# Second mixer of a two-layer step: order of the projections, and its two attentions in one alternating pipeline

## The chip, the core and the metric

The kernel runs on one core of a Trainium2 chip. The core has a matrix engine (TensorE, PE, with its weight loads PEld), a vector engine (VectorE, DVE), a scalar engine with lookup functions (ScalarE, ACT), a general engine (GpSimd, POOL) and an engine that mostly issues transfers (SyncE, SP). Each runs its own instructions in a fixed order and waits for the others through semaphores. The metric is the device time of one execution in microseconds, taken as the median of repeated runs.

## What is computed

One step of a hybrid backbone with two layers, in float32, on 384 tokens of width 1024: 128 prompt tokens, which see only each other, and 256 sample tokens, which see a cached context of 128 keys and themselves. Layer 0 mixes with windowed attention (A) and a gated scan (B); layer 1, which the change touches, mixes with latent attention (C) and with attention over normalised queries and keys (D). Behind each mixer stand an output projection with a residual layer norm and a SwiGLU feed-forward. The second mixer, cut from the reference:

```python
def mixer_cd(h, ...):
    cq, ckv, kpe, qd, kd, vd = jnp.split(h @ w_in, ODD_SPLIT, axis=-1)   # 384, 256, 32, 512, 256, 256
    qc = (rms_norm(cq, g_cq) @ w_q_up).reshape(bsz, l, 8, 64 + 32)
    ckv = rms_norm(ckv, g_ckv)
    qd = rms_norm(qd.reshape(bsz, l, 8, 64), g_dq)
    kd = rms_norm(kd.reshape(bsz, l, 4, 64), g_dk)
    # sample tokens: rotary on qc's last 32, kpe, qd, kd; context of 128 cached tokens appended to latents, keys, values
    # C: keys and values of 8 heads from (ckv @ w_kv_up), kpe shared by the heads; scores over 96 dimensions
    # D: 8 query heads of 64 on 4 key/value heads
    oc, od = dense_gqa(qc, kc, vc), dense_gqa(qd, kd, vd)    # softmax(q k^T * scale) v
    return jnp.concatenate([oc, od], -1) @ w_out
```

## The kernel before

**Precision.** A float32 product of a projection is made by three matmuls: each operand is split into a high and a low part (`wh`, `wl` of weights, `hH`, `hL` of activations). `mm3` (L126 to L129) issues high by high, low weight by high, high by low. `wload` (L113 to L124) loads a block of weights (`wr`, three buffers), makes `wh` on ACT (L122) and `wl` on DVE (L123; three buffers each). Scores, products with V and transposes are single float32 matmuls.

**Tiling.** The 384 tokens are three tiles of 128: tile 0 is the prompt, 1 and 2 the sample. A projection of n columns (`proj_all`) keeps one accumulator per token tile in PSUM and runs over the 1024 inputs in eight blocks: 72 matmuls of n columns each. PSUM has eight banks: four for `pst` (scores, transposed probabilities, D's query accumulators), three for `pjt` (projections, transposes of keys and latents), one for `pat` (products with V).

**The second mixer** (`mixer_cd`, from L1240). `acc0`, the projection of D's keys and values, comes in finished or nearly so from the boundary before it. Then, in program order:
- `acc1`, the projection of D's queries (512 columns).
- `evac_dkv` (L1282) of each tile: squares and their sum, 1/rms by a power on POOL (L110), the normalised key (L1287), for sample tiles the rotation (a product on POOL, L752; on DVE a product, L754, and an add that also doubles each head, L758), then four transposes `tk` (`turn_k`, L794), whose copies go to `kD`.
- `d_ctx`: the cached keys and values of D.
- `evac_dq` (L1295): copy, squares, rotation, four transposes `tq`, copy into `qD`; the query's 1/rms goes into the scale of the exponentials.
- the query latent, 384 columns (`proj_tm` with `evac_cq`: copy and squares on ACT, L1354 and L1355, three transposes, gain, split), and the kv latent, 288 columns (`c_ctx_`, `evac_ckv`, transposes `tl`).
- `kv_up` (keys and values of C from its latents), D's attention, `q_up` (queries of C, two halves of four heads, with the transposes `tqc`, L1405), C's attention, and `out_first`, the first half of the output projection on 512 columns.

**The attention** (L725) yields five units: one for the prompt, and one for each of four pairs of heads over the two sample query tiles. A sample unit has two parts. `pair_1` makes four score tiles of 128x384 in the `pst` banks (L722 for D, L1411 for C), their maxima (DVE, L640), exponentials with row sums (ACT, L643), reciprocals, and scales the probabilities by them (POOL, L650). `pair_2` transposes twelve blocks (L673), copies them out (L656), makes six products with V (L679) and splits the result into `hH` and `hL`. The second part of a unit is issued behind the first part of the next one.

**What sets the order.** The instructions of each engine are placed by a scheduler, which follows the program and a priority. `with ahead(part)` moves the priority of all that it encloses by the number of `part` in the table `AHEAD` (L30): a positive number moves it ahead. So pieces of D's attention (`attD`, 100) and of `q_up` (1000) stand among the projections around them. Work tiles come from pools (`Slots`): `qS` holds query buffers of 1536 columns, two of them before; `qD` takes one for the whole mixer, and the two halves `qT` of C's queries need one each.

Of the kernel before, what the change touches and what calls it, by code (L numbers as in the profile page):

```python
# [21 lines left out]
D = 1024  # L22
# [4 lines left out]
GRID_W = 64  # L27
NEG = -1e30

AHEAD = {"w": 1500, "w0": -700, "lv0": 1000, "lv1": 800, "attA": 1500, "attC": 400, "attD": 100, "fin": 500, "qs": -1500,  # L30
         "ada": -400, "ada_step": -500, "of0": -500, "of1": 1500, "ho0": 300, "ho1": 300, "gb": 100, "ib": -60,
         "kvup": 30, "cq": -200, "dctx": -100, "lat": -400, "chain": -700, "qup": 1000, "rope": 1000, "adav": -500,
         "of2": -200, "adav1": -100}

ADA = (([(0, 2), (0, 3), (0, 4)], [(0, 5, 0), (1, 0, 1), (1, 1, 0), (1, 2, 1), (1, 3, 0), (1, 4, 1)]), ([], [(1, 5, 0)]))
# [6 lines left out]
def tile_backbone_step(ctx, tc, I, O):  # L42
# [33 lines left out]
    @contextmanager  # L76
    def ahead(part, more=0):
        with tc.high_priority(offset=AHEAD[part] + more):
            yield
# [293 lines left out]
    def proj_all(w, c0, n, bank=None):  # L373
        acc, part, load = proj_parts(lambda ks: w[ks, c0:c0 + n], n, bank)
        for u in range(4):
            load(u)
            for t in range(3):
                part(t, u)
        return acc

    def proj_tm(w, c0, n, evac):
        acc = proj_all(w, c0, n)
        for t in range(3):
            evac(t, acc[t])
# [233 lines left out]

    def inv_sums(M, A, sm, nm, sink, n):
        if A.sink:  # L620
            es = M.sm.tile([P, n], F32, tag=f"es{n}", name="es")
            nc.vector.tensor_tensor(out=es.rearrange("p (a b) -> p a b", a=2), in0=nm, in1=sink, op=ALU.add)
# [6 lines left out]

    def pair_1(M, i, A):  # L630
        pr = [M.tile("pr", F32).rearrange("p (t k) -> p t k", t=2) for _ in range(2)]
# [90 lines left out]
            nc.tensor.matmul(outs[a], q[rows], k[rows], start=True, stop=stop)  # L722


    def attention(M, A):  # L725
        work = [(prompt_1, prompt_2, 0)] + [(pair_1, pair_2, i) for i in range(4)]
        prev = None
        for f1, f2, h in work:
            pr = f1(M, h, A)
            if prev:  # L730
                prev[0](M, prev[1], A, prev[2])
            prev = (f2, h, pr)
            yield
        prev[0](M, prev[1], A, prev[2])
        yield

    def drain(*gens):
        gens = list(gens)
        while gens:
            for g in list(gens):  # L740
                if next(g, 1):
                    gens.remove(g)
# [497 lines left out]
    def mixer_cd(ps1, acc0):  # L1240
        w = I["w_in_cd"][0]
        SC_D = 64 ** -0.5
        SC_C = 96 ** -0.5
        es = ExitStack()
        M = Slots(es, {"m4": (4, 1152), "u2": (3, 512), "t2": (5, 512), "one": (1, 0), "m8": (3, 2048), "qS": (2, 1536),
                       "pr": (4, 768), "pt": (6, 512), "sc": (1, 0)})
        vD = M.one.tile([P, 4, 4, 64], F32, name="vD")
        scl = {}
# [16 lines left out]
        def d_ctx():  # L1265
            kcx = dups(M, 4)
            for i in range(2):
                dma(out=kcx[0][0][:, :, i, :], in_=I["cache_d_k"][0, 0])
            dma(out=vD[:, 3], in_=I["cache_d_v"][0, 0])
            turn_k(kcx, kD, slice(384, 512), pjt)  # L1270
# [24 lines left out]
        def evac_dq(t, acc):  # L1295
            qn = M.tile("t2", F32).rearrange("p (h d) -> p h d", h=8)
            nc.scalar.activation(qn, acc.rearrange("p (h d) -> p h d", h=8), AF.Copy)
            ss = head_ss(acc, 8)
            if t:
                rope_apply(M, qn, 8, 64, tbq, t - 1, qn, False)  # L1300
            else:
                nc.vector.tensor_tensor(out=qn, in0=qn, in1=C["gdq"].unsqueeze(1).to_broadcast([P, 8, 64]), op=ALU.mult)
            turn_q(qn, qD, tok(t))
            with ahead("qs"):
                query_scale("D", t, ss, 1.0 / 64, SC_D)
# [115 lines left out]
        kT = [t8(F32, f"kT{i}") for i in range(2)]  # L1421
        latH, latL = [M.tile("m4", F32R)[:, 0:1024].rearrange("p (k n) -> p k n", k=2) for _ in range(2)]
        cqH, cqL = [M.tile("m4", F32R).rearrange("p (k n) -> p k n", k=3) for _ in range(2)]
        acc1 = proj_all(w, 672, 512, pst)
        for t in range(3):
            evac_dkv(t, acc0[t])
        d_ctx()
        for t in range(3):
            evac_dq(t, acc1[t])
        with ahead("cq"):  # L1430
            proj_tm(w, 0, 384, evac_cq)
        with ahead("lat"):
            c_ctx_()
            proj_tm(w, 384, 288, evac_ckv)
        with ahead("kvup"):
            vC = kv_up()
        with ahead("attD"):
            drain(attention(M, Att(sd_sample, sd_prompt, lambda tl, h: vD[:, tl, h // 2, :], 4,
                                   sc=scl["D"][0], nsc=scl["D"][1], nh=8, bank=pat)))
        qT = [M.tile("qS", F32).rearrange("p (h t) -> p h t", h=4) for _ in range(2)]  # L1440
        with ahead("qup"):
            q_up()
        with ahead("attC"):
            drain(attention(M, Att(sc_sample, sc_prompt, lambda tl, h: vC[:, tl, h * 64:(h + 1) * 64], 0,
                                   sc=scl["C"][0], nsc=scl["C"][1], bank=pat)))
        with ahead("of1"):
            first = out_first(I["w_out"][1], ORDER[1], keep)
# [4 lines left out]
    def ada_later(l):  # L1452
        todo = ADA[l][0]
        for i, a in enumerate(todo):
            with ahead("ada", AHEAD["ada_step"] * i):
                ada_chunk(*a)
# [79 lines left out]
```

## Time and profile before

| | |
|---|---|
| Median of three runs | 1082.47 us (1077.73 to 1084.74) |
| The profiled execution, its own time | 1080.16 us |
| Its span in the trace | 1078.3 us |
| Mean granted clock of PE | 0.989 |
| Busy: PE, DVE, ACT, POOL | 95%, 61%, 41%, 11% |

The profile is one execution. Its page gives, among others, the busy time of each engine, the chain of work that ended last, and groups of instructions by line. The trace behind it can be asked for timelines of an engine, for the busy time in chosen stretches, and for the clock that was granted to PE. A matmul counts as busy from its issue to its modelled end, so neighbours overlap in the timeline; the distance of starts is the pace. Times are counted from the span's start; the second mixer lies from about 608 to 773 us.

### The profile page before, as it was taken

The numbers are of one execution on the slowest core, as the hardware profiler recorded it, in microseconds if no ns is written. First come the engines' busy times: TensorE is split into PE (matmuls) and PEld (weight loads), VectorE is DVE, ScalarE is ACT, GpSimd is POOL, SyncE is SP. The second block draws the span as 40 slices with busy tenths as digits, with TensorE's granted clock in tenths as the row PEclk, the third lists the DMA queues.
The fourth block names the chain that finished last, engine by engine and source line by source line (L and its number), as shares of the span: only waits on it lengthen the run. The fifth ranks groups of instructions, "written<-read, shape, count | busy, mean of one in ns | idle before, by whom it ended". The sixth has DMA issues, their size and how long they took to land.

```text
span 1078.3 us, 15811 instructions
## 1 busy us (share of the span) xinstructions
PE 1023.6 (95%) x6105; PEld 865.2 (80%) x6105; DVE 657.7 (61%) x1110; ACT 440.5 (41%) x776; POOL 121.2 (11%) x166
## 2 busy tenths in 40 slices
PE   5999999997899999999999998979899999999995
PEld 4889877565799899897688776665689999998885
DVE  2589767455897477377247867656499464443337
ACT  2376746333443333232134457555163333332231
POOL 0021201210300000000001243122130000000004
PEclk8999999999999999999999999989999999999998
DMA  9873254457257777766663621144136464543331
GB/s 306 261 229 96 84 194 148 128 166 254 79 176 229 262 205 234 233 202 224 219 198 105 188 66 61 34 156 157 40 114 198 122 192 137 164 129 129 126 117 59
DMA packets 114353, 173.12 MB, mean 161 GB/s; under 512 B 9419, under 2 KB 82150, under 8 KB 114278
## 3 DMA queue, kind: packets, MB, share of 16 engines
q1 hardware_dynamic: 113526, 171.78, 50.7%
q8 instruction: 48, 0.79, 0.3%
q10 hardware_dynamic: 752, 0.34, 0.1%
q14 instruction: 27, 0.22, 0.1%
HBM read 167.84 MB, written 4.24 MB: 160 GB/s over the span
## 4 chain that ended last, share of the span: by engine, by line
PE 75%; DVE 9%; DMA 8%; issue 3%; ACT 2%; POOL 2%; SPq 0%; DVEq 0%; ACTq 0%; POOLq 0%
PE pf L129 10%; PE pf L128 10%; PE pf L127 10%; PE o L127 6%; PE o L128 6%; PE o L129 6%; DMA ar<-in_w_ada 4%; PE pj L129 3%; PE pj L127 3%; PE pj L128 3%; PE ada_acc L203 3%; DVE wl L123 2%; PE hs L883 2%; PE s L722 2%; PE ov L679 1%
## 5 line engine op out<-in xcount | busy, mean ns | idle before, releaser
L123 DVE TENSOR_TENSOR wl<-wr,wh 128x1024 fp32r<-128x1024 f32 (+4 forms) x200 | 235.9, 1182 | 239.9 <-ACT wh L122 237.1
L122 ACT ACTIVATE wh<-wr 128x1024 fp32r<-128x1024 f32 (+4 forms) x200 | 202.4, 1015 | 345.0 <-PE pf L128 123.5
L129 PE MATMUL pf<-hH,wl 128*128 128x384 f32 x688 | 232.7, 338 | 0.0
L127 PE MATMUL pf<-hH,wh 128*128 128x384 f32 x688 | 232.4, 338 | 0.0
L128 PE MATMUL pf<-hL,wh 128*128 128x384 f32 x688 | 232.4, 338 | 0.0
L129 PEld LDWEIGHTS pf<-hH,wl 128*128 128x128 f32 x688 | 129.4, 188 | 3.1 <-issue 3.1
L128 PEld LDWEIGHTS pf<-hL,wh 128*128 128x128 f32 x688 | 129.4, 188 | 2.5 <-issue 2.5
L127 PEld LDWEIGHTS pf<-hH,wh 128*128 128x128 f32 x688 | 129.4, 188 | 2.3 <-issue 2.2
L127 PE MATMUL o<-wh,aH 128*128 128x512 f32 (+1 forms) x280 | 101.3, 362 | 0.4 <-DVE a L1182 0.4
L128 PE MATMUL o<-wl,aH 128*128 128x512 f32 (+1 forms) x280 | 101.2, 361 | 0.4 <-DVE wl L123 0.4
L129 PE MATMUL o<-wh,aL 128*128 128x512 f32 (+1 forms) x280 | 101.0, 361 | 0.0
L129 PE MATMUL pj<-wh,hL 128*128 128x512 f32 (+3 forms) x240 | 88.9, 372 | 1.9 <-POOL hL L344 1.7
L127 PE MATMUL pj<-wh,hH 128*128 128x512 f32 (+3 forms) x240 | 89.2, 376 | 0.4 <-DVE vT L174 0.2
L261 DVE SCALAR_TENSOR_TENSOR part<-ar,cT,part 128x512 f32<-128x512 f32 x112 | 80.4, 747 | 13.7 <-DMA ar<-in_w_ada 13.6
L128 PE MATMUL pj<-wl,hH 128*128 128x512 f32 (+3 forms) x240 | 88.7, 370 | 0.0
L110 POOL TENSOR_TENSOR ve<-ve,nhalf 128x1 f32<-128x1 f32 x12 | 7.0, 585 | 631.7 <-DVE ve L530 370.2
L127 PEld LDWEIGHTS o<-wh,aH 128*128 128x128 f32 x280 | 52.9, 189 | 10.1 <-issue 1.4
L129 PEld LDWEIGHTS o<-wh,aL 128*128 128x128 f32 x280 | 52.8, 188 | 9.2 <-issue 1.2
L128 PEld LDWEIGHTS o<-wl,aH 128*128 128x128 f32 x280 | 52.9, 189 | 8.8 <-DVE wl L123 0.7
L129 PEld LDWEIGHTS pj<-wh,hL 128*128 128x128 f32 x240 | 45.1, 188 | 12.0 <-POOL hL L344 2.6
L127 PEld LDWEIGHTS pj<-wh,hH 128*128 128x128 f32 x240 | 44.8, 188 | 9.7 <-issue 1.9
L128 PEld LDWEIGHTS pj<-wl,hH 128*128 128x128 f32 x240 | 45.2, 188 | 7.8 <-issue 1.0
(325 smaller groups left out, 1511.5 us busy)
## 6 DMA issues: line engine op xcount, KB each, us to landing
ar<-in_w_ada SPq DMA_DIRECT2D x80, 512.0 KB
wr<-in_w_ffn_down SPq DMA_DIRECT2D x44, 512.0 KB
wr<-in_w_ffn_gate SPq DMA_DIRECT2D x40, 512.0 KB
wr<-in_w_ffn_up SPq DMA_DIRECT2D x40, 512.0 KB
wr<-in_w_in_ab SPq DMA_DIRECT2D x18, 512.0 KB
ar<-in_w_ada SPq DMA_DIRECT2D x32, 256.0 KB
wr<-in_w_out SPq DMA_DIRECT2D x16, 512.0 KB
wr<-in_w_in_ab SPq DMA_DIRECT2D x16, 256.0 KB
```

The lines of the kernel that those rows point to most:

```text
L110: nc.gpsimd.tensor_tensor(out=out, in0=v, in1=nhalf[:, :n], op=ALU.pow)
L122: nc.scalar.activation(hi, raw, AF.Copy)
L123: nc.vector.tensor_tensor(out=lo, in0=raw, in1=hi.bitcast(F32), op=ALU.subtract)
L127: nc.tensor.matmul(out, lh, rh, start=start, stop=False)
L128: nc.tensor.matmul(out, lh, rl, start=False, stop=False)
L129: nc.tensor.matmul(out, ll, rh, start=False, stop=stop)
L203: nc.tensor.matmul(acc[32 * g:32 * g + 32], st, src[:, :, g * P:(g + 1) * P], start=start, stop=stop, tile_position=(0, 32 * g))
L261: nc.vector.scalar_tensor_tensor(out=dst, in0=raw[:, j], scalar=sc, in1=dst, op0=ALU.mult, op1=ALU.add)
L679: nc.tensor.matmul(ov[64 * a:64 * a + 64], A.v(kc + 1, 2 * i + a), pt[a, kc], start=(kc == 0), stop=(kc == 2))
L722: nc.tensor.matmul(outs[a], q[rows], k[rows], start=True, stop=stop)
L883: nc.tensor.matmul(pp[:, b, :], Kc(b0 + b), Qc(b0 + b), start=True, stop=True)
```

## The change

Four numbers of the table change: `attD` 100 to 400, `cq` -200 to 0, `lat` -400 to 0, `qup` 1000 to 300. `attention` takes several attentions and alternates their units: D's prompt, C's prompt, D's first pair, C's first pair, and so on; the second part of each unit is still issued behind the first part of the next one, which is now of the other attention. `mixer_cd` makes the keys of D first, then both latents, then `acc1`, then `kv_up`, `q_up`, and both attentions in one. `qS` has three buffers. Code behind L722 stands one line later.

```diff
--- before.py
+++ after.py
@@ -27,9 +27,9 @@
 GRID_W = 64
 NEG = -1e30
 
-AHEAD = {"w": 1500, "w0": -700, "lv0": 1000, "lv1": 800, "attA": 1500, "attC": 400, "attD": 100, "fin": 500, "qs": -1500,
+AHEAD = {"w": 1500, "w0": -700, "lv0": 1000, "lv1": 800, "attA": 1500, "attC": 400, "attD": 400, "fin": 500, "qs": -1500,
          "ada": -400, "ada_step": -500, "of0": -500, "of1": 1500, "ho0": 300, "ho1": 300, "gb": 100, "ib": -60,
-         "kvup": 30, "cq": -200, "dctx": -100, "lat": -400, "chain": -700, "qup": 1000, "rope": 1000, "adav": -500,
+         "kvup": 30, "cq": 0, "dctx": -100, "lat": 0, "chain": -700, "qup": 300, "rope": 1000, "adav": -500,
          "of2": -200, "adav1": -100}
 
 ADA = (([(0, 2), (0, 3), (0, 4)], [(0, 5, 0), (1, 0, 1), (1, 1, 0), (1, 2, 1), (1, 3, 0), (1, 4, 1)]), ([], [(1, 5, 0)]))
@@ -722,16 +722,17 @@
             nc.tensor.matmul(outs[a], q[rows], k[rows], start=True, stop=stop)
 
 
-    def attention(M, A):
-        work = [(prompt_1, prompt_2, 0)] + [(pair_1, pair_2, i) for i in range(4)]
+
+    def attention(M, *As):
+        work = [(prompt_1, prompt_2, 0, A) for A in As] + [(pair_1, pair_2, i, A) for i in range(4) for A in As]
         prev = None
-        for f1, f2, h in work:
+        for f1, f2, h, A in work:
             pr = f1(M, h, A)
             if prev:
-                prev[0](M, prev[1], A, prev[2])
-            prev = (f2, h, pr)
+                prev[0](M, *prev[1:])
+            prev = (f2, h, A, pr)
             yield
-        prev[0](M, prev[1], A, prev[2])
+        prev[0](M, *prev[1:])
         yield
 
     def drain(*gens):
@@ -1242,7 +1243,7 @@
         SC_D = 64 ** -0.5
         SC_C = 96 ** -0.5
         es = ExitStack()
-        M = Slots(es, {"m4": (4, 1152), "u2": (3, 512), "t2": (5, 512), "one": (1, 0), "m8": (3, 2048), "qS": (2, 1536),
+        M = Slots(es, {"m4": (4, 1152), "u2": (3, 512), "t2": (5, 512), "one": (1, 0), "m8": (3, 2048), "qS": (3, 1536),
                        "pr": (4, 768), "pt": (6, 512), "sc": (1, 0)})
         vD = M.one.tile([P, 4, 4, 64], F32, name="vD")
         scl = {}
@@ -1421,27 +1422,26 @@
         kT = [t8(F32, f"kT{i}") for i in range(2)]
         latH, latL = [M.tile("m4", F32R)[:, 0:1024].rearrange("p (k n) -> p k n", k=2) for _ in range(2)]
         cqH, cqL = [M.tile("m4", F32R).rearrange("p (k n) -> p k n", k=3) for _ in range(2)]
-        acc1 = proj_all(w, 672, 512, pst)
         for t in range(3):
             evac_dkv(t, acc0[t])
-        d_ctx()
-        for t in range(3):
-            evac_dq(t, acc1[t])
         with ahead("cq"):
             proj_tm(w, 0, 384, evac_cq)
         with ahead("lat"):
             c_ctx_()
             proj_tm(w, 384, 288, evac_ckv)
+        acc1 = proj_all(w, 672, 512, pst)
+        d_ctx()
+        for t in range(3):
+            evac_dq(t, acc1[t])
         with ahead("kvup"):
             vC = kv_up()
-        with ahead("attD"):
-            drain(attention(M, Att(sd_sample, sd_prompt, lambda tl, h: vD[:, tl, h // 2, :], 4,
-                                   sc=scl["D"][0], nsc=scl["D"][1], nh=8, bank=pat)))
         qT = [M.tile("qS", F32).rearrange("p (h t) -> p h t", h=4) for _ in range(2)]
         with ahead("qup"):
             q_up()
-        with ahead("attC"):
-            drain(attention(M, Att(sc_sample, sc_prompt, lambda tl, h: vC[:, tl, h * 64:(h + 1) * 64], 0,
+        with ahead("attD"):
+            drain(attention(M, Att(sd_sample, sd_prompt, lambda tl, h: vD[:, tl, h // 2, :], 4,
+                                   sc=scl["D"][0], nsc=scl["D"][1], nh=8, bank=pat),
+                               Att(sc_sample, sc_prompt, lambda tl, h: vC[:, tl, h * 64:(h + 1) * 64], 0,
                                    sc=scl["C"][0], nsc=scl["C"][1], bank=pat)))
         with ahead("of1"):
             first = out_first(I["w_out"][1], ORDER[1], keep)
```

PE, behind the last matmul of `acc0` (`pj_5692` is its accumulator of tile 2, `pj_5809` and `pj_5823` those of `acc1`, `pj_6049` and `pj_5877` of the query latent). Before:

```order
L129 MATMUL pj_5692<-wh,hL 128x512
L127 MATMUL pj_5809<-wh,hH 128x512
L128 MATMUL pj_5809<-wl,hH 128x512
...
L129 MATMUL pj_5823<-wh,hL 128x512
L794 MATMUL tk<-ident,t_5915 128x128 x4
L794 MATMUL tk<-ident,t_5934 128x128 x4
L794 MATMUL tk<-ident,t_5957 128x128 x4
L785 MATMUL tq<-ident,t_5981 128x128 x4
L794 MATMUL tk<-ident,t_5970 128x128 x4
L127 MATMUL pj_6049<-wh,hH 128x384
```

After:

```order
L129 MATMUL pj_5692<-wh,hL 128x512
L795 MATMUL tk<-ident,t_5816 128x128 x4
L795 MATMUL tk<-ident,t_5835 128x128 x4
L795 MATMUL tk<-ident,t_5858 128x128 x4
L127 MATMUL pj_5877<-wh,hH 128x384
L128 MATMUL pj_5877<-wl,hH 128x384
```

The three groups of key transposes stood behind the 72 matmuls of `acc1`; now they follow `acc0` directly, and the query latent's 72 matmuls stand behind them.

DVE, at D's keys (`t_5932` and `t_5955` before, `t_5833` and `t_5856` after, are the keys of tiles 1 and 2; `ssd` their sums of squares, `wl` the low parts of weights). Before:

```order
L1290 TENSOR_TENSOR t_5911<-t_5911,gdk 128x256
L123 TENSOR_TENSOR wl<-wr,wh 128x1024
L1276 TENSOR_REDUCE ssd<-t_5924 128x4
L1232 TENSOR_SCALAR ssd<-ssd 128x4
L1287 TENSOR_TENSOR t_5932<-pj_5649,rds 128x256
L123 TENSOR_TENSOR wl<-wr,wh 128x768
L754 TENSOR_TENSOR t_5932<-t_5932,tb 128x256
L758 TENSOR_TENSOR t_5934<-t_5932,t_5935 128x512
...
L1287 TENSOR_TENSOR t_5955<-pj_5692,rds 128x256
L123 TENSOR_TENSOR wl<-wr,wh 128x768
L754 TENSOR_TENSOR t_5955<-t_5955,tb 128x256
L758 TENSOR_TENSOR t_5957<-t_5955,t_5958 128x512
```

After:

```order
L1291 TENSOR_TENSOR t_5812<-t_5812,gdk 128x256
L1277 TENSOR_REDUCE ssd<-t_5825 128x4
L1233 TENSOR_SCALAR ssd<-ssd 128x4
L656 COPY k_5796<-tk 128x2x128
L1288 TENSOR_TENSOR t_5833<-pj_5649,rds 128x256
L755 TENSOR_TENSOR t_5833<-t_5833,tb 128x256
L759 TENSOR_TENSOR t_5835<-t_5833,t_5836 128x512
...
L1288 TENSOR_TENSOR t_5856<-pj_5692,rds 128x256
L755 TENSOR_TENSOR t_5856<-t_5856,tb 128x256
L759 TENSOR_TENSOR t_5858<-t_5856,t_5859 128x512
L656 COPY k_5796<-tk 128x2x128
L123 TENSOR_TENSOR wl<-wr,wh 128x768
```

The three splits of weights that stood in the chain of the keys now stand behind it, and the copies of the transposed keys stand in it.

PE, in the sample units (`pr` are probabilities, `pt` their transposes; `m_` names are C's keys and values, `k_5796` and `vD` D's, `o_` the first half of the output projection). Before, two C units that follow one another:

```order
L673 MATMUL pt<-ident,pr 128x128 x12
L1411 MATMUL s<-m_5798,qS 128x384 x2
L679 MATMUL ov<-pt,m_6382 64x256 x4
L1411 MATMUL s<-m_5798,qS 128x384
L679 MATMUL ov<-pt,m_6382 64x256 x2
L1411 MATMUL s<-m_5798,qS 128x384
L673 MATMUL pt<-ident,pr 128x128 x8
L127 MATMUL o_7202<-wh,hH 128x512
```

After:

```order
L673 MATMUL pt<-ident,pr 128x128 x4
L679 MATMUL ov<-pt,m_6382 64x256 x4
L1412 MATMUL s<-m_5797,qS 128x384 x3
L679 MATMUL ov<-pt,m_6382 64x256 x2
L1412 MATMUL s<-m_5797,qS 128x384
L673 MATMUL pt<-ident,pr 128x128 x12
L679 MATMUL ov<-pt,vD 64x256 x4
L722 MATMUL s<-k_5796,qS 128x384 x2
L679 MATMUL ov<-pt,vD 64x256 x2
L722 MATMUL s<-k_5796,qS 128x384 x2
```

Units of C and D now stand in turn: the last products of a C unit beside the scores of C's next pair, then the transposes and products of a D unit beside the scores of D's next pair. Before, the scores beside a C unit's products were always C's.

## Rows read from the trace of the kernel before

**Rows 1.** The page: its head, busy times of engines, chain that ended last.

```profile
span 1078.3 us, 15811 instructions
...
PE 1023.6 (95%) x6105; PEld 865.2 (80%) x6105; DVE 657.7 (61%) x1110; ACT 440.5 (41%) x776; POOL 121.2 (11%) x166
...
PE 75%; DVE 9%; DMA 8%; issue 3%; ACT 2%; POOL 2%; SPq 0%; DVEq 0%; ACTq 0%; POOLq 0%
```

**Rows 2.** Stretches: from:to, length, busy of PE, PEld, DVE, ACT, POOL, clock, DMA, GB/s.

```profile
607.90:624.70 16.80, 16.80 (x74) 13.49 (x73) 11.78 (x23) 4.49 (x9) 5.80 (x7) 1.00 0.64 198
624.70:702.00 77.30, 70.03 (x439) 55.29 (x438) 51.35 (x119) 48.68 (x126) 25.79 (x37) 1.00 0.16 49
702.00:715.60 13.60, 11.00 (x68) 9.14 (x65) 9.88 (x20) 5.82 (x10) 4.21 (x6) 1.00 0.49 170
715.60:719.00 3.40, 0.01 (x1) 0.02 (x1) 3.40 (x8) 0.37 (x1) 0.11 (x1) 0.54 0.79 255
719.00:722.60 3.60, 3.59 (x9) 2.87 (x10) 1.36 (x3) 2.80 (x10) 0.00 (x0) 0.50 0.38 139
722.60:757.90 35.30, 33.54 (x169) 20.25 (x167) 18.48 (x38) 20.86 (x54) 11.86 (x18) 1.00 0.40 135
757.90:773.20 15.30, 13.10 (x63) 9.05 (x62) 4.55 (x7) 3.25 (x5) 0.33 (x1) 1.00 0.06 14
sum 165.30, PE 148.08 PEld 110.11 DVE 100.80 ACT 86.28 POOL 48.11; mean PE 21.15 PEld 15.73 DVE 14.40 ACT 12.33 POOL 6.87
```

**Rows 3.** Timeline of PE: start, length, engine, line, operation, tile, records; behind `acc1`.

```profile
624.69 1.47 PE L794 MATMUL tk<-ident,t 128*128 128x128 f32 x12
626.00 0.62 PE L785 MATMUL tq<-ident,t 128*128 128x128 f32 x4
```

**Rows 4.** Timeline of DVE at the keys; in brackets idle time before, and its releaser.

```profile
613.38 1.23 DVE L123 TENSOR_TENSOR wl<-wr,wh 128x1024 fp32r<-128x1024 f32 x1 [0.53 <-ACT wh L122]
...
617.42 1.05 DVE L123 TENSOR_TENSOR wl<-wr,wh 128x768 fp32r<-128x768 f32 x1 [0.73 <-ACT wh L122]
...
621.59 0.95 DVE L123 TENSOR_TENSOR wl<-wr,wh 128x768 fp32r<-128x768 f32 x1
...
623.77 0.69 DVE L758 TENSOR_TENSOR t<-t,t 128x512 f32<-128x512 f32 x1
```

**Rows 5.** Timeline of PE at its longest wait in the mixer.

```profile
719.01 0.42 PE L1405 MATMUL tqc<-ident,u 128*96 128x128 f32 x1 [3.40 <-DVE nm L613]
```

**Rows 6.** Groups, 604 to 775: line, operation, count, busy, mean ns, idle before, releasers.

```profile
L650 POOL TENSOR_SCALAR pr<-pr,rd 128x384 f32<-128x384 f32 x32 | 20.5, 659 | 35.5 <-DVE rd L626 26.5 <-PE ov L679 5.9 <-PE tl L1319 3.0
...
L640 DVE TENSOR_REDUCE mx<-s 128x1 f32<-128x384 f32 x32 | 17.3, 550 | 8.0 <-PE s L1411 4.6 <-PE s L722 3.1
...
L643 ACT ACTIVATE pr<-s,nm,scC 128x384 f32<-128x384 f32 x16 | 10.6, 669 | 5.2 <-DVE nm L613 5.2
...
L1354 ACT ACTIVATE u<-pj 128x384 f32<-128x384 f32 x3 | 1.6, 518 | 0.0
...
L1355 ACT ACTIVATE u<-pj 128x384 f32<-128x384 f32 x3 | 1.5, 508 | 0.0
```

**Rows 7.** Timeline of ACT: ends of the exponentials of three C units.

```profile
739.14 0.20 ACT L643 ACTIVATION_READ_ACCUMULATOR pr<-s,nm,scC 128x1 f32 x1
...
748.34 0.21 ACT L643 ACTIVATION_READ_ACCUMULATOR pr<-s,nm,scC 128x1 f32 x1
...
755.37 0.21 ACT L643 ACTIVATION_READ_ACCUMULATOR pr<-s,nm,scC 128x1 f32 x1
```

**Rows 8.** Timeline of PE: scores and products with V; two records for one score matmul.

```profile
671.76 1.56 PE L722 MATMUL s<-k,qS 64*128 64x384 f32 x8
673.25 1.52 PE L679 MATMUL ov<-pt,vD 128*64 128x256 f32 x12
...
739.39 1.56 PE L1411 MATMUL s<-m,qS 96*128 96x384 f32 x4
740.88 0.44 PE L679 MATMUL ov<-pt,m 128*64 128x256 f32 x2
```

## The prediction

> **What bounds the kernel now.** I read the page first: TensorE (PE) is busy for 95% of a span of 1078.3 us, VectorE (DVE) for 61%, and the chain that ended last runs through PE for three quarters of the span [rows 1]. So a change pays only where it takes time off PE, and the question is how much of PE's time in the second mixer is not work. The reader should then look at the busy times by stretch [rows 2]. The projection of D's keys and values (`acc0`) ends at 607.9, the output projection at about 773.2; between them lie 165.3 us, and outside them no engine's order changes. In this stretch PE is busy for 148.1 us, but a busy PE is not a PE at its rate, so I counted the work.
>
> The 72 matmuls of 512 columns of `acc1` take 16.8 us [rows 2], 0.233 each; those of 384 and 288 columns I take in proportion, 0.175 and 0.131. A 128x128 transpose takes 0.109 (twelve in 1.31 us, from the start of `tk` to the start of `tq`) [rows 3]. The scores of one D unit (a pair of heads, two query tiles) take 1.49, its products with V 1.45 (twelve in about that), two of a C unit's four scores 1.49, so a C unit's 2.98 [rows 8]. With 12 transposes, a D unit is then 4.25 us of PE work and a C unit 5.7. Summed over what stands there:
> - 607.9 to 624.7, `acc1`: 16.8 of 16.8. Nothing lost.
> - 624.7 to 702.0 (the two latent projections 22.0, `kv_up` 11.2, half of `q_up` 4.7, 105 transposes 11.4, all D scores 7.1, all D products 6.9): 63.3 of 77.3. Lost 14.0.
> - 702.0 to 719.0 (the other half of `q_up`, 16 transposes, C's prompt scores 2.2 and two scores): 10.2 of 17.0. Lost 6.8, and half of it is one wait of 3.40 us [rows 5].
> - 719.0 to 773.2 (C's other scores 10.4, 60 transposes 6.5, products 6.9, some 85 output matmuls 19.8): 43.6 of 54.2. Lost 10.6; 1.8 of it because the granted clock stands at 0.50 for 3.6 us after that wait [rows 2].
>
> Together 31.4 us are lost. No matmul goes away with the change and none comes, so the sum is: what is lost after it, against 31.4.
>
> **The change, part by part.**
>
> *D's query projection no longer stands behind the keys.* This is the largest term, and a loss. In PE's order three groups of key transposes (`tk`) followed the 72 matmuls of `acc1`; now they follow `acc0` directly, and the first latent projection stands behind them. A transpose needs the normalised, rotated key of its token tile, and the three tiles are made one after the other by ScalarE (ACT), DVE and POOL. In the trace that chain ended at 624.46, when the last add ends [rows 4], and PE came to it at 624.69: `acc1` hid all of it. Now PE arrives at 607.9. The chain itself gets shorter: three splits of weights that lie in it on DVE, at 613.38, 617.42 and 621.59 (1.23, 1.05 and 0.95 us) [rows 4], are behind it in the new order, and the splits ahead of it have 768 columns in place of 1024. Some of these splits lie in waits for POOL, so I take 2.5 of 3.2 us and put the end at 621.9. PE then waits from 607.9 to 621.9 less 0.9 for two groups of transposes: 13.1. A PE that idles so long falls to half clock: after 3.4 us without work the granted clock is 0.54 in the wait and 0.50 for 3.6 us behind it [rows 2, 5], so 1.8 more. **Lost 15**, where before nothing was; 12 if all the splits were in the way and the clock falls late, 17 if the chain is no shorter.
>
> *The latents first, then `acc1`, then `kv_up`.* Behind the keys stand 72 + 72 + 72 + 48 dense matmuls with four seams. (1) Between the query latent and the kv latent: nine transposes need a copy and a square of each of three tiles on ACT (0.52 and 0.51) [rows 6], and the three banks they write are those that the copies free; a weight split for the kv latent stands in the middle of ACT's queue. With two copies, two squares, the split and two short hops to DVE and back I get 3.3 us of wait; the context load, which now stands behind two weight loads on SP's queue, ends about when it is needed. (2) Behind the kv latent stands `acc1`, 16.8 us, which needs none of the latents: its cover hides their normalisation wholly. (3) Behind `acc1`, `kv_up` stands behind the transposes of D's second query tile, whose copy, rotation on POOL and two DVE steps start 1.4 us before `acc1` ends: 2.2 of wait, and 0.5 for the third tile. (4) The exponentials of D's prompt unit now stand on ACT ahead of the copy that frees a bank for `kv_up`'s second half: 1.1. **Lost 7** in place of 14.0, since D's units no longer lie between the projections. Bounds: 3 (only seam 1) to 11 (each other seam costs as much).
>
> *`q_up`.* Same instructions, with pieces of prompt units between its halves. The transpose that waited 3.40 us stands again ahead of output matmuls that are ready, behind splits and copies on DVE. **Lost 5** in place of 6.8 (between 3 and 7). The third query buffer frees `q_up` from waiting for D's units to be done with theirs; it moves no work.
>
> *Both attentions as one pipeline.* D and C units alternate, but one unit is still worked behind one other, with the same four score banks and four `pr` buffers. A unit's pace is set by PE's work or by the loop scores, maximum, exponentials, next scores. The exponentials of the C units end at 739.3, 748.5 and 755.6 [rows 7]: 9.2 us with output matmuls between, 7.1 with none but with a weight split in ACT's queue. Per unit, four maxima (0.55 each), four exponentials (0.67) and four products on POOL (0.66) are needed [rows 6]: 2.2, 2.7 and 2.6 us, all under PE's 4.25 and 5.7, mean 5.0. I walked four steps in the new order with these durations and got 4.2, 6.2, 6.9 and 4.5 us, mean 5.4: 0.4 over PE's work for each of 8 units, 3.2. Ahead of the first unit stand C's prompt exponentials and two weight splits, 3.5; the tail stays as it was, 1.8 (PE idles for 2.2 in the last stretch [rows 2]). **Lost 8.5** in place of 10.6. Bounds: 5.5 (5.0 a step, PE alone) and 20.5 (7.1 a step over seven steps, the C rows as they are).
>
> Sum: 15 + 7 + 5 + 8.5 = 35.5 against 31.4, so 4 us more: 1080.2 (the profiled execution, 2 us over its span) becomes 1084. The median of the runs is 1082.5, 2.3 above the profiled execution, so in its terms **1087 us**.
>
> One rule speaks for more. In the woven stretch from 624.7 to 702.0 PE idles for 7.3 us in pieces, and the granted clock stays at 1.00 [rows 2]: there is no half clock to win back by laying dense work together, and in the sum this is 0. The Trainium skill (TensorE: Matmul & The Clock Gate, "HAM oscillation — how this bites in real kernels") says that a PE which waits between bursts of matmuls is put back to half clock again and again, and advises to put the dense work in one piece. By that rule three waits at 1.8 each would be returned and the sum would be 1082; the trace does not agree here, and the new order adds one long wait ahead of the dense piece.
>
> **Rivals.** *The pipeline runs at 7.1 a step.* Each unit's scores wait for the banks of the unit before, and pairing D with C changes nothing in that. For it: the C rows ran at 7.1 to 9.2. Against it: a D unit needs 1.5 us less of PE. It gives 12 us more, 1099. Over 6.3 us a step the kernel is more than 1% slower. Chance 0.26, with the longer seams counted in.
> *The seams are hidden and the pipeline is bound by PE alone.* 12 + 3 + 3 + 5.5 = 23.5, 8 us less than before, 1074.5; to be 1% faster (1071.6) a wait would have to vanish besides. For it: most seams are estimates of short chains. Against it: the wait for the keys alone costs half of what was lost. With all that ends faster by 1%: 0.08.
> *By the clock rule* above, 1082: 0.02, within 1%.
> *The change does not do what it says*: excluded, since the rows of the order show D and C units in turn and the dense block in one piece.
>
> **How the numbers follow.** About 1% (10.8 us) is what a measurement of this kernel can tell from no change. The forecast with its neighbours inside 1% has 0.66, slower 0.26, faster 0.08. The range goes from the sum with every lower bound (1075) to the slow pipeline (1099), opened by 1 us for the spread of the runs: 1074 to 1100; I leave 2 in 10 outside.
>
> **What would show it.** Right: in the new profile PE waits for a DVE add (L759, the rotated keys) some 4 to 5 us three times behind `acc0`, with a granted clock of about 0.5 at the start of the query latent; then 200 matmuls with PE idle for under 7 us and a clock of 1.00; and exponentials ending every 5 to 6 us for the eight sample units. Wrong: a key wait under 8 us, a clock that stays at 1.00 there, or unit steps of 7 us.

## The result and the profile after

The changed kernel takes 1100.29 us (1098.72 to 1100.62) against 1082.16 us of the kernel before in the same comparison: a ratio of 1.0159, 95% interval 1.0131 to 1.0186, slower by 1.6%. The forecast was 1087 us and within 1%. The time is 0.3 us above the upper end of its range; slower by more than 1% had been given a chance of 0.26, on the rival with the slow pipeline (1099).

The profiled execution has this span, these busy times and this chain (the page's head, part 1 and part 4):

```profile
span 1098.8 us, 15814 instructions
...
PE 1034.0 (94%) x6105; PEld 873.8 (80%) x6105; DVE 656.5 (60%) x1110; ACT 443.2 (40%) x776; POOL 117.0 (11%) x166
...
PE 73%; DVE 10%; DMA 9%; issue 3%; ACT 2%; POOL 2%; SPq 0%; ACTq 0%; DVEq 0%; POOLq 0%
```

The span is 20.5 us longer than in [rows 1], with the same 6105 matmul records, and PE is busy for 10.4 us more. All but 0.4 us of it lies in the second mixer (20.1, below). The first row here is PE's wait for `hL` (the low parts of the activations) within `acc0`, before the change and after it; the distance from there to the end of the span is 483.9 us before (1078.3 less 594.42) and 504.1 after (1098.8 less 594.67), 20.2 more. Timelines of PE, the kernel before and then the changed one:

```profile
594.42 0.51 PE L129 MATMUL pj<-wh,hL 128*128 128x512 f32 x1 [0.92 <-POOL hL L344]
```

```profile
594.67 0.50 PE L129 MATMUL pj<-wh,hL 128*128 128x512 f32 x1 [0.90 <-POOL hL L344]
```

The second mixer by its new stages; columns as in [rows 2]. The stretches are: keys and query latent; kv latent; `acc1`; `kv_up` and half of `q_up`; the rest of `q_up` with the prompt units; sample units and output projection (`tc`, `tl`, `tk`, `tq`, `tqc` are transposes, `nm` the negated and scaled row maxima):

```profile
608.30:638.50 30.20, 17.95 (x84) 17.18 (x85) 11.59 (x25) 6.46 (x15) 5.40 (x8) 0.72 0.30 89
638.50:656.60 18.10, 13.70 (x87) 12.92 (x86) 8.25 (x20) 8.27 (x20) 1.37 (x3) 0.81 0.27 78
656.60:673.40 16.80, 16.80 (x75) 13.50 (x74) 8.51 (x18) 7.10 (x14) 2.62 (x6) 1.00 0.49 155
673.40:698.00 24.60, 21.49 (x117) 18.45 (x116) 16.40 (x39) 17.18 (x43) 11.10 (x13) 0.93 0.09 25
698.00:721.70 23.70, 19.18 (x109) 15.31 (x106) 14.09 (x29) 11.57 (x31) 5.67 (x8) 0.86 0.39 134
721.70:793.70 72.00, 67.88 (x352) 39.80 (x351) 40.84 (x84) 37.84 (x89) 18.80 (x33) 1.00 0.22 75
sum 185.40, PE 156.99 PEld 117.15 DVE 99.67 ACT 88.41 POOL 44.95; mean PE 26.17 PEld 19.52 DVE 16.61 ACT 14.74 POOL 7.49
```

The sum row against that of [rows 2]: the mixer is 20.1 us longer; PE idles 28.4 us in place of 17.2 (11.2 more), and is busy for 157.0 in place of 148.1 with the same work (8.9 more). The second part is mostly the clock. The same span cut where the granted clock changes:

```profile
611.80:628.90 17.10, 8.35 (x29) 7.58 (x30) 5.77 (x15) 2.88 (x8) 3.76 (x6) 0.50 0.19 65
...
642.50:649.40 6.90, 4.90 (x21) 4.84 (x22) 1.01 (x5) 0.67 (x2) 0.54 (x1) 0.51 0.20 70
...
676.70:680.10 3.40, 3.03 (x13) 2.87 (x14) 3.35 (x10) 1.94 (x4) 3.03 (x3) 0.50 0.03 5
...
714.20:721.00 6.80, 4.73 (x12) 3.80 (x13) 2.18 (x8) 4.64 (x19) 0.90 (x2) 0.50 0.25 95
```

For 34.2 us PE has half its clock, in four stretches, with 21.0 us of busy time in them; half of that, 10.5, is time that full clock would not need. Before it was one stretch with 3.6 busy [rows 2], 1.8. PE's waits from 605 to 795 (engine, what waits, for what: us in total, times, longest):

```profile
PE tk L795 <- DVE t L759: 7.5, 2, 4.1
PE tk L795 <- ACT t L779: 4.7, 1, 4.7
PE tl L1319 <- DMA u<-in_cache_c_kv: 3.0, 1, 3.0
PE tqc L1406 <- DVE nm L613: 2.6, 1, 2.6
PE tl L1319 <- DVE u L1341: 2.4, 1, 2.4
PE pt L673 <- ACT pr L643: 2.2, 3, 1.1
```

The keys' transposes `tk` wait 12.2 us. Before, those of the three token tiles followed `acc1` without a wait [rows 3] and the longest wait in the mixer was that of `tqc`, 3.40 [rows 5]. The row for `u` L1341 is the kv latent of the third tile: PE waits 2.4 us for it right behind `acc1`, which was to hide it.

### The profile page after: what moved, and what is told of

Read it like the earlier page. It is cut to its first block, busy times and chain, and to the rows that moved or that the text cites. A ratio compares the mean times of both kernels' runs of the same rounds, so it can differ in the third digit from the quotient of the medians.

```text
span 1098.8 us, 15814 instructions
## 1 busy us (share of the span) xinstructions
PE 1034.0 (94%) x6105; PEld 873.8 (80%) x6105; DVE 656.5 (60%) x1110; ACT 443.2 (40%) x776; POOL 117.0 (11%) x166
## 4 chain that ended last, share of the span: by engine, by line
PE 73%; DVE 10%; DMA 9%; issue 3%; ACT 2%; POOL 2%; SPq 0%; ACTq 0%; DVEq 0%; POOLq 0%
PE pf L129 9%; PE pf L127 9%; PE pf L128 9%; PE o L127 6%; PE o L128 6%; PE o L129 6%; DMA ar<-in_w_ada 5%; PE pj L127 4%; PE pj L129 4%; PE pj L128 4%; PE ada_acc L203 3%; DVE wl L123 2%; PE hs L884 2%; DMA wr<-in_w_in_ab 2%; PE s L722 2%
## 5 line engine op out<-in xcount | busy, mean ns | idle before, releaser
L261 DVE SCALAR_TENSOR_TENSOR part<-ar,cT,part 128x512 f32<-128x512 f32 x112 | 80.4, 748 | 13.2 <-DMA ar<-in_w_ada 13.1
L129 PEld LDWEIGHTS pj<-wh,hL 128*128 128x128 f32 x240 | 46.7, 195 | 11.2 <-POOL hL L344 2.4
```

Of the source, the lines that this page charges most:

```text
L129: nc.tensor.matmul(out, ll, rh, start=False, stop=stop)
L261: nc.vector.scalar_tensor_tensor(out=dst, in0=raw[:, j], scalar=sc, in1=dst, op0=ALU.mult, op1=ALU.add)
```

## The experiments

Each kernel is the changed one with a small edit, unless said otherwise. The table gives the median, the ratio to the kernel before with its interval, and, from the profile, the distance from the `hL` wait to the end of the span against 483.9 of before. This distance leaves out the first 594 us: the row of the wait stands between 591.7 and 599.4 in these profiles, though the edits lie behind it, so a single span carries several us of the part ahead. The distance comes from one profile of each kernel, and it does not always agree with the ratio: b3 has the time of the kernel before (0.9996) and a distance of +2.8, and against the changed kernel e5, e6 and b1 gain 4.7 to 5.1 us more in the distance than in the ratio (taken of 1082 us); in their profiles the wait stands 2.9 to 4.8 us later than in the changed kernel's. Whether that is chance or comes with the edit stays open, and small differences in the distance alone show little.

| kernel | median us | ratio (95%) | distance |
|---|---|---|---|
| changed | 1100.29 | 1.0159 (1.0131 to 1.0186) | +20.2 |
| e1_q_first | 1089.35 | 1.0044 (1.0025 to 1.0063) | +7.8 |
| e2_two_att | 1098.09 | 1.0125 (1.0096 to 1.0154) | +16.7 |
| e3_ctx_early | 1097.13 | 1.0109 (1.0078 to 1.0139) | +15.5 |
| e4_cq_cover | 1087.14 | 1.0030 (1.0011 to 1.0050) | +5.2 |
| e5_staged | 1098.91 | 1.0147 (1.0122 to 1.0171) | +14.2 |
| e6_u2 | 1101.85 | 1.0184 (1.0159 to 1.0209) | +17.8 |
| e7_warm | 1099.01 | 1.0157 (1.0133 to 1.0181) | +18.3 |
| e8_small | 1098.55 | 1.0151 (1.0134 to 1.0169) | +20.0 |
| b1 | 1088.85 | 1.0049 (1.0025 to 1.0073) | +3.2 |
| b2 | 1076.11 | 0.9957 (0.9944 to 0.9970) | -2.9 |
| b3 | 1080.59 | 0.9996 (0.9980 to 1.0012) | +2.8 |
| b4 | 1076.51 | 0.9961 (0.9945 to 0.9978) | -3.9 |

**The cover ahead of the keys.**

```diff
+        acc1 = proj_all(w, 672, 512, pst)
         for t in range(3):
             evac_dkv(t, acc0[t])
...
-        acc1 = proj_all(w, 672, 512, pst)
```

> The changed kernel with one line moved back: D's query projection (acc1, 72 matmuls, 16.8 us) stands again ahead of D's keys; latents, q_up and the alternating pipeline stay as changed. Theory (the three waits for keys and the half clock behind them cost 16 us, because nothing stands ahead of them): all 16 come back, and the latents' normalisation, which has lost its cover, costs 2 to 4 new: 1086 to 1089 us. Rival (what PE waits for is a chain through DVE and ACT that only moves along): 1095 to 1100 us.

Measured: 12.4 us less in the distance, and 1.1% in the ratio; the median, 1089.35, is 0.4 us above what the theory named. PE's waits in this kernel:

```profile
PE tl L1319 <- DMA u<-in_cache_c_kv: 3.0, 1, 3.0
PE tqc L1406 <- DVE nm L613: 2.6, 1, 2.6
PE tl L1319 <- DVE u L1341: 2.3, 1, 2.3
PE pt L673 <- ACT pr L643: 2.2, 3, 1.1
PE tl L1319 <- DVE pe L762: 1.8, 1, 1.8
PE vn L127 <- ACT m L1322: 1.7, 1, 1.7
```

The `tk` rows are gone; two new ones of 1.8 and 1.7 us stand behind the kv latent, which lost the cover of `acc1`. So here one projection hides only one of the two chains, and the change moved it from the longer to the shorter. The other way is to take another projection:

```diff
+        accq = proj_all(w, 0, 384, pst)
         for t in range(3):
             evac_dkv(t, acc0[t])
         with ahead("cq"):
-            proj_tm(w, 0, 384, evac_cq)
+            for t in range(3):
+                evac_cq(t, accq[t])
```

> The changed kernel with the query latent's projection (72 matmuls of 384 columns, 12.6 us) put ahead of D's keys, into the banks that D's queries take later; all else as changed. Theory (any dense projection that stands ahead of the keys hides their chain, up to its own length): 12 to 14 us come back, the transposes of the query latent find their data ready: 1084 to 1088 us. Rival (the splits of these weights stand again in the chain of the keys on DVE and lengthen it by 3 us or more): 1089 to 1093 us.

Measured: 15.0 us less in the distance, and 1087.14 us, as the theory had it. Of the waits for the keys one is left:

```profile
PE tk L795 <- DVE t L759: 2.8, 1, 2.8
PE tqc L1406 <- DVE nm L613: 2.6, 1, 2.6
PE tl L1319 <- DVE u L1341: 2.4, 1, 2.4
PE tl L1319 <- DMA u<-in_cache_c_kv: 2.3, 1, 2.3
```

The two runs show that most of the loss, 12.4 to 15.0 of 20.2 us, hangs on what stands ahead of the keys. The order of the parts need not be that of before.

**Why the chain of the keys is so long.** ACT's timeline at the keys in the changed kernel:

```profile
605.54 0.39 ACT L1275 ACTIVATE t<-pj 128x256 f32<-128x256 f32 x1 [0.55 <-PE pj L129]
605.82 0.38 ACT L1284 ACTIVATE vD<-pj 128x256 f32<-128x256 f32 x1
612.34 0.63 ACT L779 ACTIVATE t<-t 128x512 f32<-128x512 f32 x1 [6.14 <-DVE t L1291]
612.88 0.37 ACT L1275 ACTIVATE t<-pj 128x256 f32<-128x256 f32 x1
```

ACT idles 6.14 us at L779, the copy of the prompt tile's finished key; the squares of tile 1 (L1275), for which only `acc0` is needed, stand behind it. The Trainium skill ("TensorE: Matmul & The Clock Gate", section "Architectural detail: the array is 16× 32×32, not 1× 128×128") says that ScalarE and VectorE keep strictly to the order of their queues, and this row agrees. So the squares and 1/rms of all three tiles (`dkv_sums`, the first lines of the old `evac_dkv`, into tiles of their own) were put ahead; in the same edit the copy of the values into `vD` (L1284) and its store moved behind each tile's transposes:

```diff
+        rds = [dkv_sums(t, acc0[t]) for t in range(3)]
         for t in range(3):
-            evac_dkv(t, acc0[t])
+            evac_dkv(t, acc0[t], rds[t])
...
```

> The changed kernel with the keys of D made in stages: squares, sums and 1/rms of all three token tiles first, then normalising, rotation and transposes of each, so that a tile's chain no longer starts behind the one before it. Theory (the second and third wait, 4.1 and 3.4 us, are the chain of one tile standing in the queues behind the chain of another): about 5 of these 7.5 come back, and a little of the half clock: 1093 to 1095 us. Rival (the chain is bound by the work of DVE and POOL, not by the order of the tiles): 1098 to 1100 us.

```profile
PE tk L795 <- ACT t L779: 5.1, 1, 5.1
PE tl L1327 <- DMA u<-in_cache_c_kv: 3.1, 1, 3.1
PE tk L795 <- DVE t L759: 2.9, 2, 1.7
```

The second and third wait fell from 7.5 to 2.9 us and the distance by 6.0: the chains did stand in each other's way. The median fell by less than the theory asked (1098.91, the rival's number), and the two intervals together allow anything from some 5 us faster than the changed kernel to 3 us slower; in this profile the `hL` wait stands 3.3 us later than in the changed kernel's. How much it is worth in the whole time stays open, and so does the share of the moved copies.

The first wait did not shrink (4.7, then 5.1 us). In the changed kernel DVE works there on the layer norm of the part before (L405, L406), between the steps of tile 0's key; from 608.03 to the key's last step at 611.89 five such instructions start:

```profile
607.70 0.41 DVE L1277 TENSOR_REDUCE ssd<-t 128x4 f32<-128x256 f32 x1
608.03 0.68 DVE L406 TENSOR_TENSOR x<-x,lnb 128x512 f32<-128x512 f32 x1
...
611.29 0.68 DVE L406 TENSOR_TENSOR x<-x,lnb 128x512 f32<-128x512 f32 x1
611.89 0.42 DVE L1291 TENSOR_TENSOR t<-t,gdk 128x256 f32<-128x256 f32 x1
```

No run here moved them.

**The price of the half clock.** Matmuls that nobody reads fill the three waits:

```diff
+        wm, prev = pst("wm"), [lastmm[0].ins]
         for t in range(3):
+            with tc.issue_after(prev[-1]):
+                for _ in range((22, 18, 15)[t]):
+                    nc.tensor.matmul(wm[:, :NTOK], hH[:, 7, 2 * P:3 * P], hH[:, 7, :], start=True, stop=True)
...
```

> The changed kernel with 55 extra matmuls of 384 columns into a bank that nobody reads, 22, 18 and 15 of them ahead of the three groups of key transposes, where PE waits 4.7, 4.1 and 3.4 us. The waits stay, but PE is busy in them. Theory (behind the waits the half clock costs 4 us of the 16.3 lost there): the granted clock stays at 1.00 and the time falls to 1095 to 1097 us. Rival (the clock falls whatever stands in the waits, or its price is hidden): 1099 to 1102 us; more than that if the extra matmuls delay the transposes.

Busy times over the stretch that had 0.50 in the changed kernel:

```profile
611.80:628.90 17.10, 13.79 (x82) 12.87 (x81) 5.92 (x15) 3.08 (x9) 3.79 (x6) 1.00 0.20 67
```

The clock stays at 1.00 here, so PE's idleness in the waits was what took it. But the distance falls by 1.9 us only, and the ratio is that of the changed kernel: the clock did as the theory said, the time as the rival. The keys end 0.2 us earlier, their last transposes starting at 622.54 in place of 622.75, and the last matmul of the query latent starts 2.8 us earlier (635.58 against 638.37). Behind it some of that is lost again, for instance in two new waits at a prompt unit, 1.5 us together (`pt` for POOL's `pr`). So of the 10.5 us of the half clock the part behind the keys (half of 8.35, 4.2) is worth about 2 us in this profile, and the ratios do not tell it from nothing.

**The late load of the cached latents.** The buffer and its two loads stand at the mixer's start, behind that of `vD`:

```diff
+        lcx = M.one.tile([P, 288], F32, name="lcx")
+        dma(out=lcx[:, 0:256], in_=I["cache_c_kv"][0, 0])
...
-            lcx = M.tile("u2", F32)[:, 0:288]
-            dma(out=lcx[:, 0:256], in_=I["cache_c_kv"][0, 0])
...
```

> The changed kernel with the cached latents of C loaded at the mixer's start into a buffer of their own, so that PE does not wait 3.0 us for that transfer between the two latent projections. Theory (this wait, and the 6.8 us at half clock behind it, are on the path): 1094 to 1097 us. Rival (the same transposes would wait almost as long for their bank, whose copies stand in ACT's queue): 1098 to 1101 us.

The wait of 3.0 us is gone from this kernel's waits, and the granted clock stays at 1.00 there (from 640 to 650). The distance falls by 4.7: wait and half clock behind it, as the theory had it; the median, 1097.13, is 0.1 us above what it named.

**Buffers.** Five `u2` buffers in place of three, and three small ones in place of two:

> The changed kernel with five in place of three buffers of the pool u2, from which the normalised kv latents, their rotation products and C's queries come. Theory (the third tile's latent waits for a buffer that only transposes behind acc1 give back, 2.45 us of PE and half clock behind it; and q_up's last transpose, 2.64 us and half clock, waits for a buffer of the same pool): 1092 to 1096 us. Rival 1 (only the latent does): 1096 to 1098 us. Rival 2 (neither; the queues' order does it): 1099 to 1101 us.

> The changed kernel with three in place of two buffers for each small tile (sums, 1/rms, the rotated key part of the kv latent). In the order of the instructions this alone moves the multiply that makes the third tile's latent from behind acc1's evacuations up to the other two. Theory (the 2.45 us wait of PE behind acc1 is that late multiply): the wait and the half clock behind it go, 3 to 4 us, the rest stays: 1096 to 1098 us. Rival (the transposes then wait as long for something else there, a copy or a bank): 1099 to 1101 us.

Both reasons failed. With five `u2` buffers the waits for `u L1341` and `nm L613` stand unchanged at 2.4 and 2.6; what shrank is the wait for the cached latents, 3.0 to 1.3, whose load takes its buffer from the same pool. The median, 1101.85, is above all three ranges, while the distance fell by 2.4. With three small buffers the late multiply did go, but a `tk` wait took its place:

```profile
PE tqc L1406 <- DVE nm L613: 2.6, 1, 2.6
PE pt L673 <- ACT pr L643: 2.1, 3, 1.1
PE tk L795 <- issue: 1.7, 1, 1.7
```

The distance falls by 0.2 us, as its rival said; the median, 1098.55, lies between the two ranges.

**The alternating units.**

```diff
-                                   sc=scl["D"][0], nsc=scl["D"][1], nh=8, bank=pat),
-                               Att(sc_sample, sc_prompt, lambda tl, h: vC[:, tl, h * 64:(h + 1) * 64], 0,
+                                   sc=scl["D"][0], nsc=scl["D"][1], nh=8, bank=pat)))
+        with ahead("attC"):
+            drain(attention(M, Att(sc_sample, sc_prompt, lambda tl, h: vC[:, tl, h * 64:(h + 1) * 64], 0,
```

> The changed kernel with two attentions, one behind the other (all of D, then all of C), in place of the alternating pipeline; projections as changed. Theory (a sample unit takes 6.7 us because of the loop of scores, maximum, exponentials and banks, alternating or not): 1098 to 1103 us. Rival (alternating is itself the loss, for instance by a worse mix on PE): 1090 to 1095 us. Second rival (alternating helped much): over 1106 us.

Measured: 3.5 us less in the distance, 0.3% in the ratio, with intervals that overlap; the median is at the lower edge of the first theory. In its waits the row `tqc <- nm L613` is missing: without alternation C's prompt unit, whose maxima are on DVE, no longer stands ahead of `q_up`'s last transpose. The pace of a unit can't be compared well: the exponentials of the last four C units here end 7.0, 6.9 and 7.6 us apart, those of the eight alternating units 6.7 on average, but a C unit holds more PE work (5.7 us against a mean of 5.0), and output matmuls stand between the units in both. What speaks for neutral units is b4, below.

**Putting it together.** b1 is e4's cover with e3, e5 and e6 (`lcx`, stages, `u2`); b2 adds the three small buffers and the two separate attentions; b3 is the kernel *before* with `lcx`, `u2` and small buffers; b4 is b2 with alternating units again, C two units behind D:

```diff
+            d, c = units
+            work = d[:3] + [c[0], d[3], c[1], d[4]] + c[2:]
```

> The query latent's projection as cover ahead of D's keys, the cached latents loaded early, the keys in stages and five u2 buffers, all together on the changed kernel. Theory (each of these waits is on the path and they add): cover 13, load 3, latent buffer 3, stages 1 to 2 less than the changed kernel: 1078 to 1082 us, 0 to 0.5% below the kernel before. Rival (taking one wait away moves the loss to the next chain): 1084 to 1088 us.

> The kernel before with three helps that do not depend on the change: cached latents loaded early, five u2 buffers, three small buffers; order of the parts and both attentions as before. Theory (its waits of 1.0 and 1.1 us at the latents' transposes go, little else, since its projections are woven with D's units): 1079 to 1081 us. Rival 1 (the order shifts and a new wait comes): 1082 to 1086 us. Rival 2 (q_up's wait of 3.4 us goes too): 1074 to 1077 us.

> The kernel with all four helps (query latent as cover, early load, staged keys, five u2 buffers), with three small buffers as well, and with the two attentions one behind the other. Theory (each measured term adds in the second mixer's stretch: 3 us above the kernel before with the four helps, less 3.5 for two attentions, less 3 to 4 for the small buffers): 1078 to 1081 us, below the kernel before. Rival (alternating units pay once the projections are dense, and taking them away costs): 1085 to 1090 us.

> The best kernel so far (query latent as cover, early load, staged keys, five u2 and three small buffers), but with the units of both attentions in turn again, C two units behind D: D's prompt and first two pairs, C's prompt, then C and D by turns, then C's last pairs. C's prompt unit so stands behind most of q_up. Theory (alternating units is neutral for the pace of a unit; what it cost was C's prompt unit, whose maxima stood on DVE ahead of q_up's last transpose): within 2 us of that kernel with the attentions one behind the other, 1075 to 1079 us. Rival 1 (alternating is itself slower, units of D and C hinder each other): 1080 to 1084 us. Rival 2 (alternating pays 3 us or more once it starts later): under 1074 us.

b1 lost on what its parts had promised (15 + 4.7 + 6 + 2.4 would be 28 in the distance; it got 17.0; by the ratio 18 and 11.9), and its median, 1088.85, is above even its rival's range. Two of the parts, e3 and e6, had shortened the same wait, and with the cover there the stages can have little left to hide; the latter was not tested alone. b3 shows no difference: the early load and the buffers alone bring the kernel before nothing. b2 is faster than the kernel before by 0.43%, and below the range of its theory; its longest waits are short:

```profile
PE pt L673 <- ACT pt L658: 2.0, 3, 0.9
PE tk L795 <- issue: 1.6, 1, 1.6
PE o L127 <- ACT wh L122: 1.1, 1, 1.1
```

b4 has the same time with alternating units, as its theory said: they are neutral here, as long as C's prompt unit stands behind most of `q_up`. b2 and b4 beat both kernels with latents, `acc1`, `kv_up` and `q_up` in the order of the change. So that order does not have to cost: most of the loss was the missing cover, and the rest, of which e4 still shows 0.3%, goes with the helps of b2 together.

## Why the prediction was right in its mechanism and short in its sum

- **The mechanism of the largest term was right.** PE waits for the keys in the order and at the place named, 4.7, 4.1 and 3.4 us (12.2 against 13.1; the first for ACT's copy of the prompt's key, L779, where the sign named L759 for all three), and e1 and e4 bring most of it back. The lost time of that stretch is 30.2 less 13.9 of work (72 matmuls at 0.175 and 12 transposes at 0.109), 16.3 against 15. That the chain would be shorter without the weight splits was right too: it ends at 622.7, where 621.9 was said.
- **The cover of `acc1` was right for itself, not for what it hides.** It loses nothing, 16.80 busy of 16.80. But it was to hide the normalisation of the kv latents "wholly", and the third tile's latent comes late: PE waits 2.4 us for it behind `acc1`, with 3.4 us of half clock after that.
- **The seams were mis-sized, and beyond their bound:** 18.1 less 10.8 and 24.6 less 19.7 of work (48 matmuls of `kv_up`, 27 of `q_up`, 25 transposes, D's prompt scores), 12.2 against 7 (3 to 11). The steps that failed are "the context load ends about when it is needed", where PE waits 3.0 us for a load that is issued only at 641.38, and the whole cover just named, 2.4; neither had the half clock behind it in its price (6.9 and 3.4 us with 7.9 busy, 4.0). e3 took 4.7 us off at the load, and e6 points to its buffer as part of the delay.
- **`q_up`** lost 23.7 less 15.3 of work (27 of its matmuls, 32 transposes, 12 output matmuls, C's prompt scores, D's prompt products and two scores), 8.4 against 5 (3 to 7). The wait that was forecast to stay is there, shorter (2.6 against 3.40 [rows 5]), with two others of 1.1 and 0.7 and 6.8 us of half clock.
- **The half clock was counted once, at 1.8.** It came four times: 21.0 us busy at half clock. This is in the terms of the keys, the seams and `q_up`, and it is the common error: only the wait for the keys was priced with a half clock behind it. Each stretch begins within a wait of PE: at 611.8, 642.5, 676.7 and 714.2, where waits end at 613.02, 644.50, 677.07 and 716.27. The Trainium skill ("TensorE: Matmul & The Clock Gate", "HAM oscillation — how this bites in real kernels") says that a PE which waits between bursts of matmuls is put back to half clock each time; the trace agrees, with four stretches. Dense pieces of work did not prevent it here, since the waits stood ahead of the pieces.
- **The pipeline** lost 72.0 less 58.7 (74 output matmuls 17.3, 104 transposes 11.3, scores 17.1, products 13.0), 13.3 against 8.5 (5.5 to 20.5). Exponentials of the first and the last of the eight units end at 726.98 and 774.08:

```profile
726.79 0.19 ACT L643 ACTIVATION_READ_ACCUMULATOR pr<-s,nm,scD 128x1 f32 x1
...
773.88 0.20 ACT L643 ACTIVATION_READ_ACCUMULATOR pr<-s,nm,scC 128x1 f32 x1
```

  That is 47.1 us for seven steps, 6.7 each, where four walked steps had given 5.4 and the rival said 7.1. But 21 output matmuls stand in these 47.1 us (4.9 at 0.233), so without them a step is 6.0, between the two. And the rival's mechanism, scores that wait for the banks of the unit before, is not what the trace shows: PE is busy for 44.5 of the 47.1 us, and waits 2.2 of the rest for exponentials. The term was mis-sized, by 4.8 of the 14.7 us by which the sum fell short; the seams carry 5.2, `q_up` 3.4, the keys 1.3. That the time landed at the rival's 1099 is a coincidence. (The bounds 5.5 and 20.5 do not quite follow from their own terms: 3.5 and 1.8 without any loss in the steps are 5.3, and 2.1 more for each of seven steps makes 20.0.)
- **The whole:** 50.2 us lost (185.4 less 135.2) against 35.5; the counted work of the same instructions is 135.2 here and was 133.9 before, so 1.3 us of the mixer's 20.1 is the counting. Each of the four terms was too small, two of them beyond their upper bound: three of them share a cause (the half clock), so the bounds should have been added with one sign. Of the signs that were named, the three waits and the half clock behind them came; 200 matmuls at a clock of 1.00 and units of 5 to 6 us did not.

What stays open: what makes a unit longer than its counted work in either form (PE is busy for nearly all of it; the order on PE, banks and ACT were not told apart), what each of the four changed priorities does by itself, and the wait `u L1341` (L1349 there) in b1, which neither more `u2` buffers removed nor more small ones without another wait in its place.

## What to carry to other kernels

Before a projection is moved, look at what it hides where it stands: a dense block whose inputs are ready is the cover of the chain beside it, and here it was cheap to swap it for another block, but not to leave none. Price a wait of TensorE with the half clock that the trace shows behind such waits, and then take that price as an upper bound: here 4.2 us of it returned about 2. An interleaving that starts a second consumer earlier can also put its vector work ahead of the first one's.

## What the runs showed of the hardware

The two scores of a pair of D's heads use 64 rows each, on different halves of PE's rows. In [rows 8] eight records of them, four matmuls, take 1.49 us. Among products with V in the changed kernel, one that stands alone takes 0.84 us (from its start to the next, 733.88 to 734.72), and a pair that stands together takes 0.84 as well (746.50 to 747.34):

```profile
733.88 0.91 PE L722 MATMUL s<-k,qS 64*128 64x384 f32 x2
734.72 0.65 PE L679 MATMUL ov<-pt,vD 128*64 128x256 f32 x4
...
746.50 0.92 PE L722 MATMUL s<-k,qS 64*128 64x384 f32 x4
747.34 0.65 PE L679 MATMUL ov<-pt,vD 128*64 128x256 f32 x4
```

So a pair of neighbours costs what one costs alone; an order that separates them pays for it, on an engine that reads as busy. In the seven steps above two of six pairs are separated, so an estimate of the price from these rows is 1.7 us of the 13.3 lost in the sample units. The kernel before separates some of its pairs too.
